# First layer's modulation: half of the products as fp32 matmuls of 512 columns, read back from diagonals

## The chip, the cores and the metric

The kernel runs on one core of a Trainium2 chip. The metric is the device time of one execution, in microseconds (us); every text here means that time when it says "time". The engines are TensorE (PE, with its weight loads shown apart as PEld), VectorE (DVE), ScalarE (ACT), GpSimd (POOL) and SyncE (SP), which issues most DMAs.

## The reference, cut to what matters

Four layers work on `x` of 1024 tokens by 1024 features. Each layer begins with a modulation that depends on the condition `c` alone:

```
cond = jax.nn.silu(c)                                     # (1, 1024)
for i in range(DEPTH):
    mod = (cond @ w_mod[i] + b_mod[i])[:, None, :]        # w_mod[i]: 1024 x 3072
    shift, scale, gate = jnp.split(mod, 3, axis=-1)
    h = rms_norm(x, norm_pre_g[i]) * (1.0 + scale) + shift
    o = mixer_i(h, ...)                                   # GLA, SGU, FoX, GLA
    x = x + gate * rms_norm(o, norm_post_g[i])
```

The change touches only how `shift` and `scale` of the first layer are computed, a product of one row of 1024 by a matrix of 1024 x 2048 in fp32. They are needed as columns: feature on the partition, one column for each block of 128 features.

## The kernel before, in words

`setup` loads the small vectors, transposes them with PE into `vec`, and makes `cond` (128 partitions x 8 columns: feature `128 kt + p` of silu(c) on partition p of column kt).

`begin` is the first layer's start. It holds the part that changes. It goes through four blocks of 512 columns of `w_mod[0]`, in the order j = 0, 2, 1, 3. Blocks 0 and 1 are the shift (`SH`), blocks 2 and 3 the scale (`G`, which becomes (1 + scale) times the norm's weight). In the texts the four are numbered in their order of arrival, w0 to w3: w0 is SH of features 0 to 511, w1 is G of the same features, w2 and w3 are SH and G of features 512 to 1023. One block comes in four DMAs of 512 KB (kp = 0 to 3), each with two row blocks of 128 (kt = 2 kp and 2 kp + 1), into a pool `whl` of eight buffers that the projection's split weights share.

`mod_pieces` with `wide=True` does the sum over the 1024 rows of a block in two places. DVE (L264) multiplies a row block by its column of `cond` and adds it into `acc` (128 x 512, which starts as zero with the bias in row 0), so that partition p holds a partial sum; PE (L274) then sums `acc` over the partitions with a column of ones, four matmuls of one column, which lands as columns in PSUM. Every fourth row block (kp odd, i = 1) goes to PE directly (L259): four matmuls whose weights are a 128 x 128 piece of `w_mod` and whose moving operand is the one column of `cond`. All go into one PSUM tile `pt` of the pool `pb` (two buffers), opened by a product with zeros (L243).

Between the blocks `begin` starts the first four token tiles (`first`): ACT takes the mean square and scales the tile (L425, L431, with POOL's L415 and L416 between them), PE transposes it (L443), and ACT copies the two PSUM halves out (L1261) into `raw`. When `SH` and `G` of a half are there, `entry_b` applies them to the four tiles of that half (ACT L457, for features 512 to 1023 partly DVE L454), ACT rounds to `hTh` (L462) and DVE, for the last one POOL, makes the rest `hTl` (L466). The first projection (L361, L362, L363: one product in three) needs both. ACT also splits the projection's weights (`whi` L321, `wlo` L323); for some of them the second part is finished by an accumulating DMA that POOL issues (L324).

The kernel is written with a scheduler: it orders each engine's instructions itself, except those that are pinned to the program's order (ACT's instructions of the first entry among them). So an engine's order can differ from the order of the code, and every engine works its list strictly in that order.

Of the kernel before, what the change touches and what calls it, by code (L numbers as in the profile page):

```python
# [8 lines left out]
F32 = mybir.dt.float32  # L9
# [3 lines left out]
ALU = mybir.AluOpType  # L13
AX = mybir.AxisListType

P = 128
# [78 lines left out]
class Trunk:  # L95
# [39 lines left out]
    def setup(self):  # L135
        nc, cp, a = self.nc, self.cp, self.a
        self.ident = cp.tile([P, P], F32, name="ident")
        make_identity(nc, self.ident)
        self.ones = cp.tile([P, P], F32, name="ones")
        nc.vector.memset(self.ones, 1.0)  # L140
        self.zero = cp.tile([P, 4], F32, name="zero")
        nc.vector.memset(self.zero, 0.0)
        self.half = cp.tile([P, 8], F32, name="neghalf")
        nc.vector.memset(self.half, -0.5)
        self.junk = cp.tile([P, 256], mybir.dt.bfloat16, name="junk")
        L = a["norm_pre_g"].shape[0]
        self.onesr = cp.tile([P, P], F32R, name="onesr")
        nc.vector.tensor_copy(self.onesr, self.ones)
        rows = self.s2([P])
        nc.vector.memset(rows, 0.0)  # L150
        n = 0
        self.vcol = {}

        def put(key, ap, cnt):
            nonlocal n
            nc.sync.dma_start(out=rows[n:n + cnt, 0:ap.shape[1]], in_=ap)
            self.vcol[key] = n
            n += cnt


        self.xts = [self.load_x(0)]
        put("c", a["c"].rearrange("b (k p) -> (b k) p", p=P), KT)
        put("gpre", a["norm_pre_g"].rearrange("l (k p) -> (l k) p", p=P), L * KT)
        self.xts.append(self.load_x(1))
        put("ghead", a["gla_g_head"].rearrange("l h (k p) -> (l h k) p", p=P), 2 * 8)
        put("ba", a["gla_b_a"].rearrange("l (k p) -> (l k) p", p=P), 2 * 4)
        self.xts.append(self.load_x(2))
        self.vcol["gq"] = n
        nc.sync.dma_start(out=rows[n:n + 1, 0:64], in_=a["fox_g_q"])
        nc.sync.dma_start(out=rows[n:n + 1, 64:128], in_=a["fox_g_q"])  # L170
        self.xts.append(self.load_x(3))
        self.vcol["gk"] = n + 1
        nc.sync.dma_start(out=rows[n + 1:n + 2, 0:64], in_=a["fox_g_k"])
        nc.sync.dma_start(out=rows[n + 1:n + 2, 64:128], in_=a["fox_g_k"])
        n += 2
        put("bf", a["fox_b_f"], 1)
        pt = self.ps("pm")
        nc.tensor.transpose(pt[:, 0:P], rows, self.ident)
        self.vec = cp.tile([P, P], F32, name="vec")
        nc.vector.tensor_copy(self.vec, pt[:, 0:P])  # L180
        c0 = self.vcol["c"]
        th = cp.tile([P, KT], F32, name="cth")
        nc.scalar.activation(th, self.vec[:, c0:c0 + KT], AF.Tanh, scale=0.5)
        nc.vector.scalar_tensor_tensor(th, th, 1.0, self.vec[:, c0:c0 + KT], op0=ALU.add, op1=ALU.mult)
        self.cond = cp.tile([P, KT], F32, name="cond")
        nc.vector.tensor_scalar(self.cond, th, 0.5, None, op0=ALU.mult)
        g0 = self.vcol["ghead"]
        self.ghalf = cp.tile([P, 16], F32, name="ghalf")
        nc.vector.tensor_scalar(self.ghalf, self.vec[:, g0:g0 + 16], 0.5, None, op0=ALU.mult)

        self.hTh = self.hp.tile([P, KT, SEQ], F32R, name="hTh")
        self.hTl = self.hp.tile([P, KT, SEQ], F32R, name="hTl")
        self.xd = [self.dp.tile([SEQ, D], F32, name=f"xd{i}") for i in range(max(1, len(self.layers) - 1))]
        self.yd = [self.dp.tile([SEQ, D], F32, name=f"yd{i}") for i in range(len(self.layers))]
        self.G = [None] * 4
        self.SH = [None] * 4
        self.gg = [None] * 4
# [25 lines left out]
    def mod_pieces(self, l, cols, wide=False):  # L223
        nc, a = self.nc, self.a
# [5 lines left out]
        G, SH, gg = self.G[l], self.SH[l], self.gg[l]  # L230
        pieces, ends = [], []

        def col(j):
            st = {}

            def begin():
                acc = self.sp.tile([P, 512], F32, tag="md", name=self.nm("md"), bufs=4)
                nc.gpsimd.memset(acc, 0.0)
                nc.sync.dma_start(out=acc[0:1, :], in_=a["b_mod"][l:l + 1, j * 512:(j + 1) * 512])
                st["acc"] = acc  # L240
                if wide:
                    st["pt"] = self.ps("pb")
                    nc.tensor.matmul(st["pt"][:, 0:4], self.ident, self.zero, start=True, stop=False)  # L243

            def step(kp):
                w = []
                if wide:
                    wt = self.wp.tile([P, 2, 512], F32, tag="whl", name=self.nm("md2"))
                    self.last["sp"] = nc.sync.dma_start(out=wt, in_=a["w_mod"][l, 2 * kp * P:(2 * kp + 2) * P, j * 512:(j + 1) * 512]
                                      .rearrange("(i p) n -> p i n", p=P))  # L250
                    w = [wt[:, i, :] for i in range(2)]
                else:
                    for i in range(2):
                        w.append(self.sp.tile([P, 512], F32, tag="md", name=self.nm("md"), bufs=4))
                for i in range(2):
                    kt = 2 * kp + i
                    if wide and kp % 2 and i:
                        for c in range(4):
                            nc.tensor.matmul(st["pt"][:, c:c + 1], w[i][:, c * P:(c + 1) * P], self.cond[:, kt:kt + 1],  # L259
                                             start=False, stop=False)  # L260
                        continue
                    if not wide:
                        nc.sync.dma_start(out=w[i], in_=a["w_mod"][l, kt * P:(kt + 1) * P, j * 512:(j + 1) * 512])
                    ins = nc.vector.scalar_tensor_tensor(st["acc"], w[i], self.cond[:, kt:kt + 1], st["acc"],  # L264
                                                         op0=ALU.mult, op1=ALU.add)
                    if not wide:
                        self.tc.keep_in_program_order(ins)

            def finish():
                acc = st["acc"]  # L270
                if j < 4:
                    pt = st["pt"] if wide else self.ps("pm")
                    for i in range(4):
                        self.last["tensor"] = nc.tensor.matmul(pt[:, i:i + 1], acc[:, i * P:(i + 1) * P], self.ones[:, 0:1],  # L274
                                                               start=not wide, stop=not wide or i == 3)
                    k0 = (j % 2) * 4
                    if j < 2:
                        nc.vector.tensor_copy(SH[:, k0:k0 + 4], pt[:, 0:4])
                    else:
                        g0 = self.vcol["gpre"] + l * KT + k0  # L280
                        nc.vector.scalar_tensor_tensor(G[:, k0:k0 + 4], pt[:, 0:4], 1.0, self.vec[:, g0:g0 + 4],
                                                       op0=ALU.add, op1=ALU.mult)
                else:
                    cs = (j - 4) * 512
                    gp = self.s2([512])
                    nc.sync.dma_start(out=gp, in_=a["norm_post_g"][l:l + 1, cs:cs + 512].partition_broadcast(P))
                    pt = self.ps("pm")
                    hi, lo = self.s2([512], F32R), self.s2([512], F32R)
                    nc.scalar.copy(hi, acc)
                    nc.gpsimd.tensor_tensor(lo, acc, hi.bitcast(F32), op=ALU.subtract)  # L290
                    nc.tensor.matmul(pt, self.onesr, hi, start=True, stop=False)
                    nc.tensor.matmul(pt, self.onesr, lo, start=False, stop=True)
                    nc.vector.tensor_tensor(gg[:, cs:cs + 512], pt, gp, op=ALU.mult)

            pieces.append(lambda: (begin(), step(0)))
            if ends:
                pieces.append(ends.pop())
            for kp in range(1, 4):
                pieces.append((lambda kp: lambda: step(kp))(kp))
            ends.append(finish)  # L300
            if wide or j == cols[-1]:
                pieces.append(ends.pop())
# [1043 lines left out]
```

## Time and profile before

| | us |
|---|---|
| median of 3 runs | 2137.44 |
| lowest, highest | 2134.9, 2142.99 |
| the profiled execution, its own time | 2137.6 |
| its span, first to last instruction | 2135.9 |
| PE busy in the span | 2069.4 (97%) |
| DVE, ACT, POOL busy | 1242.0, 956.5, 715.9 |

"Busy" counts the records of instructions; matmuls are pipelined, so PE busy does not mean PE at its peak. The span can be cut into stretches: up to 13.5 us the small loads, to 44.2 us the modulation, to 64 us the first projection that waits for pieces of the entry, and after that a long run in which PE is rarely without work. Of an fp32 matmul the trace has two records, of a product in fp32r or a transpose one.

### The profile page before, as it was taken

To read this page: it belongs to the slowest core of one execution; us is meant where nothing else is said; L and a number is where in the kernel's file an instruction comes from. 1 tells how busy PE (TensorE), PEld (TensorE's weight loads), DVE (VectorE), ACT (ScalarE), POOL (GpSimd) and SP (SyncE) were. 2 spreads that over 40 slices of the span, in tenths; PEclk is the share of its full clock that TensorE was granted. 3 is DMA by queue.
4 is the path that set the end of the run, shared out by engine and by line. 5 is a ranking of instruction groups with operands and counts; after the bars stand their busy time and mean duration, and the time that the engine had idled before them with its cause. 6 is when DMAs were issued, how large, how long until landed. Compare 5 with 4: busy or idle time off the path is not lost. (4 is left out here: it accounts for less than half of the span.)

```text
span 2135.9 us, 35845 instructions
## 1 busy us (share of the span) xinstructions
PE 2069.4 (97%) x13637; PEld 1847.1 (86%) x13637; DVE 1242.0 (58%) x2877; ACT 956.5 (45%) x1963; POOL 715.9 (34%) x730
## 2 busy tenths in 40 slices
PE   6999999999999999999999999999899899999998
PEld 6889999988998888898888888888687799899986
DVE  5476768545375425556656656656765554766542
ACT  5556445335321114554445445445555664543331
POOL 1422222345244322535343243343223321222251
PEclk9999999999999999999999999999999999999999
DMA  8344445434425433324223224223424542333422
GB/s 294 72 122 115 126 121 144 136 112 142 127 82 158 143 109 107 125 63 109 75 75 110 80 70 110 80 70 109 136 83 144 142 98 61 89 80 94 146 94 91
DMA packets 166965, 237.29 MB, mean 111 GB/s; under 512 B 14642, under 2 KB 97138, under 8 KB 166794
## 3 DMA queue, kind: packets, MB, share of 16 engines
q1 hardware_dynamic: 160170, 210.82, 31.4%
q0 software_dynamic: 6624, 24.19, 6.4%
q8 instruction: 107, 1.75, 0.3%
q14 instruction: 64, 0.52, 0.1%
HBM read 172.44 MB, written 29.95 MB: 95 GB/s over the span
## 5 line engine op out<-in xcount | busy, mean ns | idle before, releaser
L361 PE MATMUL pj<-whi,hTh 128*128 128x256 f32 (+1 forms) x2048 | 599.4, 293 | 6.2 <-ACT s L1047 2.7
L363 PE MATMUL pj<-whi,hTl 128*128 128x256 f32 (+1 forms) x2048 | 591.5, 289 | 0.5 <-DVE hTl L466 0.4
L362 PE MATMUL pj<-wlo,hTh 128*128 128x256 f32 (+1 forms) x2048 | 591.7, 289 | 0.0
L361 PEld LDWEIGHTS pj<-whi,hTh 128*128 128x128 f32 x2048 | 394.2, 192 | 13.2 <-issue 5.3
L362 PEld LDWEIGHTS pj<-wlo,hTh 128*128 128x128 f32 x2048 | 394.0, 192 | 5.0 <-issue 2.2
L363 PEld LDWEIGHTS pj<-whi,hTl 128*128 128x128 f32 x2048 | 393.9, 192 | 5.2 <-issue 2.2
L363 PE MATMUL pj<-hTh,wlo 128*128 128x512 f32 x640 | 253.4, 396 | 2.1 <-DMA wlo<-wraw 2.1
L361 PE MATMUL pj<-hTh,whi 128*128 128x512 f32 x640 | 255.2, 399 | 0.0
L362 PE MATMUL pj<-hTl,whi 128*128 128x512 f32 x640 | 252.5, 394 | 0.0
L326 POOL TENSOR_TENSOR wlo<-wraw,whi 128x1024 fp32r<-128x1024 f32 (+2 forms) x64 | 141.2, 2216 | 154.1 <-ACT whi L321 153.9
L264 DVE SCALAR_TENSOR_TENSOR md<-md,cond,md 128x512 f32<-128x512 f32 x184 | 161.2, 877 | 39.1 <-DMA md<-in_w_mod 37.3
L1120 POOL TENSOR_TENSOR db<-s,mneg 128x128 f32<-128x128 f32 x128 | 67.8, 537 | 276.5 <-DVE mx L1135 165.3
L321 ACT CAST whi<-wraw 128x1024 fp32r<-128x1024 f32 (+2 forms) x112 | 110.7, 989 | 95.3 <-PE pj L362 70.8
L1154 ACT COPY s<-pm 128x512 f32<-128x512 f32 (+2 forms) x192 | 87.5, 480 | 126.9 <-PE pm L1152 124.0
L363 PEld LDWEIGHTS pj<-hTh,wlo 128*128 128x128 f32 x640 | 120.7, 189 | 27.3 <-DMA wlo<-wraw 2.5
L361 PEld LDWEIGHTS pj<-hTh,whi 128*128 128x128 f32 x640 | 120.8, 189 | 23.7 <-issue 0.7
L362 PEld LDWEIGHTS pj<-hTl,whi 128*128 128x128 f32 x640 | 120.8, 189 | 23.6 <-issue 0.7
L1141 ACT ACTIVATE p<-p,ng 128x256 f32<-128x256 f32 (+7 forms) x128 | 99.5, 778 | 86.1 <-DVE ng L1139 85.1
L361 PE MATMUL pj<-wo,hTh 128*128 128x512 f32 x320 | 126.4, 396 | 1.7 <-ACT s L496 1.7
L362 PE MATMUL pj<-wo,hTh 128*128 128x512 f32 x320 | 125.2, 391 | 0.0
L363 PE MATMUL pj<-wo,hTl 128*128 128x512 f32 x320 | 123.5, 392 | 0.0
L1130 DVE CUSTOM_DVE_ANT_0 p<-pb,s 128x512 f32<-128x512 f32 (+3 forms) x160 | 82.4, 527 | 62.1 <-PE pb L1127 59.3
(223 smaller groups left out, 4072.7 us busy)
## 6 DMA issues: line engine op xcount, KB each, us to landing
md<-in_w_mod SPq DMA_DIRECT2D x160, 256.0 KB
wlo<-wraw POOLq DMA_DIRECT2D x44, 512.0 KB, 5.2
wraw<-in_gla_w_in SPq DMA_DIRECT2D x32, 512.0 KB
yd<-s SPq DMA_DIRECT2D x50, 256.0 KB
xd<-x SPq DMA_DIRECT2D x24, 512.0 KB
wraw<-in_sgu_w_in SPq DMA_DIRECT2D x24, 512.0 KB
x<-xd SPq DMA_DIRECT2D x24, 512.0 KB
wraw<-in_fox_w_in SPq DMA_DIRECT2D x48, 256.0 KB
```

The costliest lines, as they stand in the source:

```text
L264: ins = nc.vector.scalar_tensor_tensor(st["acc"], w[i], self.cond[:, kt:kt + 1], st["acc"], op0=ALU.mult, op1=ALU.add)
L321: nc.scalar.copy(hi, raw)
L326: getattr(nc, sub).tensor_tensor(lo, raw, hi.bitcast(F32), op=ALU.subtract)
L361: nc.tensor.matmul(ps, lh, rh, start=first, stop=False)
L362: nc.tensor.matmul(ps, lh, rl, start=False, stop=False)
L363: nc.tensor.matmul(ps, ll, rh, start=False, stop=last)
L1120: nc.gpsimd.tensor_tensor(db, nf[p, ib // 4, hb][:, qc], mneg, op=ALU.add)
L1130: nc.vector.tensor_tensor_reduce(e[:, c * 512:c * 512 + d0], sp[:, 0:d0], nf[p, c, hb][:, 0:d0], op0=ALU.add, op1=ALU.max, scale=1.0, scal ...
L1141: nc.scalar.activation(e[:, 0:n + P], e[:, 0:n + P], AF.Exp, bias=ng, accum_out=ls[:, 0:1])
L1154: nc.scalar.copy(et[:, 0:nb * P], pt[:, 0:nb * P])
```

## The change

For the four blocks of the first layer, and for them only:

- `crow` is new: the columns kt = 1, 3, 5, 7 of `cond`, each repeated 128 times, 4 x 128 x 128 in all, made by one DVE copy (L187).
- Of each kp the second row block (i = 1) goes to PE, now for all four kp. It is one fp32 matmul (L258) whose weights are the repeated condition and whose moving operand is the row block, 128 x 512. Every partition of `pt` then holds the same row of 512 sums. The first one opens `pt`; the product with zeros and its tile are gone.
- `acc` gets the four first row blocks (i = 0) on DVE as before, four L262 (L264 before) in place of six.
- At the end one fp32 matmul of `ones` (128 x 128) by `acc` (L275) adds its sums to the same `pt`, in place of four of one column.
- Since `pt` holds rows, the columns are picked out: for each 128 columns DVE multiplies `pt` by the identity and sums along the row (L278, `tensor_tensor_reduce`, whose sum is written by a second instruction), into `SH` or `G`. For `G` the step with the norm's weight then works on it in place (L288).

The other layers' blocks are as before. The diff, cut to this:

```diff
+        self.crow = self.s2([4, P])
+        nc.vector.tensor_copy(self.crow, self.cond.rearrange("p (k i) -> p k i", i=2)[:, :, 1:2].to_broadcast([P, 4, P]))
...
                 if wide:
                     st["pt"] = self.ps("pb")
-                    nc.tensor.matmul(st["pt"][:, 0:4], self.ident, self.zero, start=True, stop=False)
...
-                    if wide and kp % 2 and i:
-                        for c in range(4):
-                            nc.tensor.matmul(st["pt"][:, c:c + 1], w[i][:, c * P:(c + 1) * P], self.cond[:, kt:kt + 1],
-                                             start=False, stop=False)
+                    if wide and i:
+                        nc.tensor.matmul(st["pt"], self.crow[:, kp, :], w[i], start=kp == 0, stop=False)
                         continue
...
-                    for i in range(4):
-                        self.last["tensor"] = nc.tensor.matmul(pt[:, i:i + 1], acc[:, i * P:(i + 1) * P], self.ones[:, 0:1],
-                                                               start=not wide, stop=not wide or i == 3)
...
+                    col = (SH if j < 2 else G)[:, k0:k0 + 4]
+                    if wide:
+
+                        self.last["tensor"] = nc.tensor.matmul(pt, self.ones, acc, start=False, stop=True)
+                        dg = self.s2([4, P])
+                        for i in range(4):
+                            nc.vector.tensor_tensor_reduce(dg[:, i, :], pt[:, i * P:(i + 1) * P], self.ident, op0=ALU.mult,
+                                                           op1=ALU.add, scale=1.0, scalar=0.0, accum_out=col[:, i:i + 1])
```

The scheduler's order changes with it, in the first part of each engine's list; from there on the lists are the same but for one matmul of a later modulation that moves by some rows. Three places follow.

On DVE, the end of the modulation. `md_317` and `md_328` are w2's `acc`, `md_351` and `md_368` w3's. Before:

```order
L326 TENSOR_TENSOR wlo_365<-wraw_301,whi_364 128x1088
L281 SCALAR_TENSOR_TENSOR G_148<-pb_269,vec 128x4
L264 SCALAR_TENSOR_TENSOR md_328<-md_53_333,cond,md_328 128x512
L264 SCALAR_TENSOR_TENSOR md_328<-md_54_337,cond,md_328 128x512
L264 SCALAR_TENSOR_TENSOR md_328<-md_55_344,cond,md_328 128x512 x2
```

Now, where ISA is L278, two rows for each:

```order
L262 SCALAR_TENSOR_TENSOR md_351<-md_69_363,cond,md_351 128x512
L262 SCALAR_TENSOR_TENSOR md_351<-md_70_367,cond,md_351 128x512
L278 ISA s_51_281,G_148<-pb_263,ident 128x128
L278 ISA G_148 128x1
...
L278 ISA s_60_338,SH_149<-pb_320,ident 128x128
L278 ISA SH_149 128x1
...
L288 SCALAR_TENSOR_TENSOR G_148<-G_148,vec 128x4
L473 TENSOR_TENSOR hTl<-s_22_193,hTh 128x4x128
L278 ISA s_71_372,G_148<-pb_354,ident 128x128
```

`G` of the first half (`pb_269` before, `pb_263` now) stood ahead of nearly all of w2's sums; it now stands behind the last sum of w3.

On PE, from the first of w2's products on. Before:

```order
L259 MATMUL pb_331<-cond,md_54_337 128x1 x4
L243 MATMUL pb_371<-zero,ident 128x4
L259 MATMUL pb_331<-cond,md_56_348 128x1 x4
L443 MATMUL pm_252<-ident,x_112 128x128 x4
L443 MATMUL pm_257<-ident,x_112 128x128 x4
L274 MATMUL pb_331<-ones,md_328 128x1 x4
L259 MATMUL pb_371<-cond,md_64_377 128x1 x4
```

Now:

```order
L258 MATMUL pb_320<-md_59_333,s_7_124 128x512
L450 MATMUL pm_225<-ident,x_106 128x128 x4
L450 MATMUL pm_230<-ident,x_106 128x128 x4
L275 MATMUL pb_320<-md_317,ones 128x512
L450 MATMUL pm_246<-ident,x_110 128x128 x4
L450 MATMUL pm_251<-ident,x_110 128x128 x4
L258 MATMUL pb_354<-md_67_355,s_7_124 128x512
```

(`s_7_124` is `crow`; `x_112` and `x_110` are the fourth token tile.) The first tile's transposes moved too: before they were ahead of all products of the modulation, now they come behind w1's third product.

On SP, the first loads. Before:

```order
L826 DMA s_7_140<-in_gla_w_a 16x512 x3
L239 DMA md_150<-in_b_mod 1x512
L249 DMA md_11_155<-in_w_mod 128x2x512
L249 DMA md_12_159<-in_w_mod 128x2x512
L249 DMA md_13_166<-in_w_mod 128x2x512
L249 DMA md_14_170<-in_w_mod 128x2x512
L239 DMA md_266<-in_b_mod 1x512
```

Now:

```order
L240 DMA md_150<-in_b_mod 1x512
L249 DMA md_12_154<-in_w_mod 128x2x512
L249 DMA md_13_158<-in_w_mod 128x2x512
L249 DMA md_14_162<-in_w_mod 128x2x512
L249 DMA md_15_166<-in_w_mod 128x2x512
L240 DMA md_260<-in_b_mod 1x512
L833 DMA s_8_140<-in_gla_w_a 16x512 x3
```

Three small loads (`in_gla_w_a`, which ACT's second instruction reads, ahead of the first token tile) moved from ahead of w0 to behind it; the second token tile's load moved behind two small ones.

## Rows read from the trace of the kernel before

**Rows 1.** The page's head and first part: busy time, share, instructions.

```profile
span 2135.9 us, 35845 instructions
...
PE 2069.4 (97%) x13637; PEld 1847.1 (86%) x13637; DVE 1242.0 (58%) x2877; ACT 956.5 (45%) x1963; POOL 715.9 (34%) x730
```

**Rows 2.** Windows: stretch, its length, busy by engine (instructions), clock, DMA share, GB/s.

```profile
13.50:44.20 30.70, 28.04 (x132) 27.87 (x133) 21.24 (x30) 19.54 (x31) 3.18 (x7) 1.00 1.00 334
```

**Rows 3.** Timeline of ACT: start, us, instruction, count, idle before and its releaser.

```profile
19.41 1.15 ACT L431 ACTIVATE x<-x,r 128x1024 f32<-128x1024 f32 x1 [0.95 <-POOL r L416]
...
37.83 1.65 ACT L457 ACTIVATE s<-s,SH,G 128x128 f32<-128x128 f32 x4
...
56.09 0.62 ACT L462 CAST hTh<-s 128x512 fp32r<-128x512 f32 x1
```

**Rows 4.** Timeline of POOL, end of the first entry.

```profile
56.78 1.29 POOL L466 TENSOR_TENSOR hTl<-s,hTh 128x512 fp32r<-128x512 f32 x1 [22.68 <-ACT hTh L462]
...
58.95 1.99 POOL L324 DMA_DIRECT2D wlo<-wraw  x2
```

**Rows 5.** Timeline of PE, modulation and first projection.

```profile
14.82 1.97 PE L443 MATMUL pm<-ident,x 128*128 128x128 f32 x8 [4.33 <-ACT x L431]
...
23.30 1.71 PE L259 MATMUL pb<-cond,md 128*128 128x1 f32 x8
...
35.34 1.97 PE L443 MATMUL pm<-ident,x 128*128 128x128 f32 x8 [1.05 <-ACT x L431]
...
44.61 0.43 PE L362 MATMUL pj<-wlo,hTh 128*128 128x272 f32 x1
44.84 0.43 PE L363 MATMUL pj<-whi,hTl 128*128 128x272 f32 x1
...
47.71 0.29 PE L361 MATMUL pj<-whi,hTh 128*128 128x272 f32 x1
47.83 0.29 PE L362 MATMUL pj<-wlo,hTh 128*128 128x272 f32 x1
...
63.75 0.50 PE L363 MATMUL pj<-hTh,wlo 128*128 128x512 f32 x1 [2.06 <-DMA wlo<-wraw]
...
65.32 0.63 PE L362 MATMUL pj<-hTl,whi 128*128 128x512 f32 x1
65.75 0.63 PE L363 MATMUL pj<-hTh,wlo 128*128 128x512 f32 x1
```

**Rows 6.** Timeline of DVE in the modulation.

```profile
13.57 2.33 DVE L264 SCALAR_TENSOR_TENSOR md<-md,cond,md 128x512 f32<-128x512 f32 x3 [1.24 <-DMA md<-in_w_mod]
...
18.93 2.33 DVE L264 SCALAR_TENSOR_TENSOR md<-md,cond,md 128x512 f32<-128x512 f32 x3 [0.39 <-DMA md<-in_w_mod]
...
27.86 0.75 DVE L264 SCALAR_TENSOR_TENSOR md<-md,cond,md 128x512 f32<-128x512 f32 x1 [0.37 <-DMA md<-in_w_mod]
...
40.20 1.54 DVE L264 SCALAR_TENSOR_TENSOR md<-md,cond,md 128x512 f32<-128x512 f32 x2
```

**Rows 7.** Timeline of PE later: two fp32 matmuls of 256 columns.

```profile
394.85 0.59 PE L789 MATMUL pm<-st,s 128*128 128x256 f32 x2
395.28 0.59 PE L790 MATMUL pm<-s,s 128*128 128x256 f32 x2
```

**Rows 8.** Timeline of DVE later: a multiply-and-reduce of 128 columns out of PSUM.

```profile
1442.76 0.29 DVE L1135 CUSTOM_DVE_ANT_0 p<-pb,db 128x128 f32<-128x128 f32 x1
1442.97 0.08 DVE L1135 DVE_READ_ACCUMULATOR2_ANT mx<- 128x1 f32 x1
1442.97 0.75 DVE L264 SCALAR_TENSOR_TENSOR md<-md,cond,md 128x512 f32<-128x512 f32 x1
```

**Rows 9.** Timeline of SP's queue, modulation loads.

```profile
9.31 1.93 SPq L249 DMA_DIRECT2D md<-in_w_mod  x4
...
30.57 0.37 SPq L249 DMA_DIRECT2D md<-in_w_mod  x1
...
32.93 1.75 SPq L249 DMA_DIRECT2D md<-in_w_mod  x2
```

More of the change, by code (lines that the diff above doesn't have):

```diff
@@ L140, in setup @@
         nc.vector.memset(self.ones, 1.0)
-        self.zero = cp.tile([P, 4], F32, name="zero")
-        nc.vector.memset(self.zero, 0.0)
         self.half = cp.tile([P, 8], F32, name="neghalf")
@@ L272, in finish @@
                     pt = st["pt"] if wide else self.ps("pm")
-                    for i in range(4):
-                        self.last["tensor"] = nc.tensor.matmul(pt[:, i:i + 1], acc[:, i * P:(i + 1) * P], self.ones[:, 0:1],
-                                                               start=not wide, stop=not wide or i == 3)
                     k0 = (j % 2) * 4
-                    if j < 2:
-                        nc.vector.tensor_copy(SH[:, k0:k0 + 4], pt[:, 0:4])
-                    else:
+                    col = (SH if j < 2 else G)[:, k0:k0 + 4]
[5 more added lines that the diff above has]
+                                                           op1=ALU.add, scale=1.0, scalar=0.0, accum_out=col[:, i:i + 1])
+                    else:
+                        for i in range(4):
+                            nc.tensor.matmul(pt[:, i:i + 1], acc[:, i * P:(i + 1) * P], self.ones[:, 0:1],
+                                             start=True, stop=True)
+                    if j < 2 and not wide:
+                        nc.vector.tensor_copy(col, pt[:, 0:4])
+                    elif j >= 2:
                         g0 = self.vcol["gpre"] + l * KT + k0
-                        nc.vector.scalar_tensor_tensor(G[:, k0:k0 + 4], pt[:, 0:4], 1.0, self.vec[:, g0:g0 + 4],
+                        nc.vector.scalar_tensor_tensor(col, col if wide else pt[:, 0:4], 1.0, self.vec[:, g0:g0 + 4],
                                                        op0=ALU.add, op1=ALU.mult)
```

## The prediction

> **What bounds the kernel now.** I read the page's first part first: PE is busy 2069.4 of 2135.9 us [rows 1], so outside some 66 us nothing but fewer or faster products of PE shortens the run, and the change takes no work from the long part. It acts in one place, so the rest is read there. The windows view of 13.5 to 44.2 us [rows 2] shows the modulation: PE busy 28.0 of 30.7 us, DVE 21.2, ACT 19.5, and the DMA engines at a share of 1.00 with 334 GB/s. Three things look like a bound, and the busy shares can't tell which it is.
>
> PE's busy time there is cheap work: eight records of one-column products take 1.71 us, 0.21 us each [rows 5]. The clock column says 1.00, but the durations contradict it: at 44.6 us the first products of 272 columns follow each other in 0.23 us, and at 47.7 us, after some 3 us of such products without a pause, in 0.12 us [rows 5]. [...] For PE in this stretch the durations count, not the column.
>
> DVE waits for data at each block: 13.57 (w0), 18.93 (w1), 27.86 (w2) are starts released by DMA [rows 6]. w0 to w1 is 5.36 us, 1.34 us for a DMA of 512 KB.
>
> What sets the end of the stretch is found backwards from the first long wait of PE in the projection: 2.06 us up to 63.75 for a `wlo` that an accumulating DMA finishes [rows 5]. POOL issues that DMA at 58.95, behind its `hTl` of the last tile at 56.78, which waits for ACT's last `hTh` at 56.09 [rows 3, 4]. ACT gets there by one list of modulate and round steps that begins at 37.83 and is nearly unbroken, 18.9 us to 56.7. **So the price of the change is how far the start of that list, 37.83, moves.** Behind 64 us PE is the bound and what it loses ahead it doesn't get back.
>
> **The change part by part.**
>
> *DVE's sums.* Of 24 steps of 0.75 us [rows 6], 8 go: 6.0 us less. Added are 16 multiply-and-reduce steps. The nearest rows are those of 128 columns out of PSUM with max in place of sum: 0.29 us plus 0.08 for the write of the result, and the next instruction starts 0.21 us after the first began [rows 8]. Between 0.21 and 0.37 each, 3.4 to 5.9 us; I take 0.25, since the trace's instructions overlap: 4.0 us. The net gain of DVE is 0.1 to 2.6 us, but DVE waited for data there anyway, so I count nothing for it. The copy into `crow` lies between 0.3 us and 0.75 us (a DVE pass of 512 fp32 [rows 6]); it runs while w0 is still on its way, as long as that lands after some 11.9 us.
>
> *PE's products.* Out go 32 products of one column and the 16 of the sums, 96 records of 0.21 us, 20.5 us, and 4 with zeros. In come 20 fp32 products of 512 columns. The trace has none of that width with two records; two of 256 columns start 0.43 us apart at the full clock [rows 7], so 0.86 us for 512, and at half the clock 1.71. The bill of PE is 17 us at the one and 34 us at the other level, in a stretch of 30.7 us that also holds 32 transposes (7 to 8 us at half clock, by eight records in 1.97 [rows 5]). Which level it is decides the case. These products stream columns without a pause, like those at 44.6, so I expect the rise within a few us of the first. Then each product (0.86) is shorter than its DMA (1.34), PE waits for data, and may fall back: after the 2.06 us of idling before 63.75 the products of 512 columns at 65.3 again follow each other in 0.43 us [rows 5]. It will swing, with the busy half in its favour.
>
> [...]
>
> *The loads.* The three small loads go behind w0, and w0's first DMA can go before 9.31 [rows 9]. I take 1.7 us, since `cond` and `crow` aren't there before about 11.9; the bounds are 0 and 2.3. Then w0 to w2 keep their distances, since transfers set them: w2's first piece at 26.2 in place of 27.86, its last three pitches later, 30.2. ACT's second instruction now waits for the small loads behind w0: about 16 us. So the first token tile is squared and scaled by about 20 us in place of 14.8.
>
> *ACT's tiles.* From one tile's transposes (14.82) to the next one's scaled tile it takes 5.7 us (19.41 plus 1.15 [rows 3, 5]), and the four came in 6.8 us each because PE had other work (14.82 to 35.34). Now the first transposes stand behind w1's third product, which lands near 20: 20.8. Three steps of 5.4 to 5.9 give the fourth tile's transposes at 37.1 to 38.6, in place of 35.34. They were followed by the start of ACT's list after 2.5 us (35.34 to 37.83), which is 2.0 at full clock: **39.1 to 41.1**.
>
> *G behind w3.* The other condition for that start. `G` of the first half was read long before w3's end; now its four steps and the four of w2's `SH` stand on DVE behind w3's last sum. w3's buffers come free when both DVE and PE have used w2's: first DMA issued at 30.57 before, the last by 34.7, and the last sum ended at 41.74 (40.20 plus 1.54), 7.0 us later [rows 6, 9]. Now the last goes out when w2's last product is done, 30.2 plus 0.9, and the last sum ends at 36.3 (four pitches after w2's last, and 0.75) to 38.1 (7.0 after its issue). With 8 steps of 0.25 and the small step of 0.16: **38.5 to 40.3**. The same reading frees a `pb` buffer, so w3's five products on PE can't begin before; their sums are needed only some 10 us after ACT's start, since ACT has its list of the first half ahead of them: five products of 1.71, 8.6 us, and 1.2 of DVE fit, hardly.
>
> *Sum.* ACT's list starts at the later of the two, 39.1 to 41.1; I take 40.7, near the end with PE at the lower level for part of the time, 2.9 us later than 37.83. The list keeps its 18.9 us, POOL's DMA and PE's wait go with it. What PE saves by being warm at 44 (some 1.4 us) lies ahead of pieces that it then waits for. The profiled execution took 2137.6 us; 2137.6 plus 2.9 is **2140.5 us**, slower than the median of 2137.44 by 0.14%.
>
> **The rivals.**
>
> *PE stays at its lower level (slower).* Speaks for it: it did so for 30 us with a busy share of 0.9 [rows 2]. Against: those were one-column products. Eight products of 1.71 (w0's five, w1's three) put the first transposes at 25.6, and w2's last product at 39.4, after six more products and two tiles' transposes of 1.75 each; w3's last sum ends 7.0 later, 46.4, and G is there at 48.6. The list starts 10.8 us late: 2148.4 us. It decides from the point where a product is longer than its DMA of 1.34 us for most of the 20.
>
> *The earlier loads win.* If the small loads are what held w0, and PE is warm from the first block on, both chains end at their early bounds or a little ahead, 37.0 to 39: from 0.8 us faster to 1.2 slower, 2136.8 to 2138.8. No path gives more, since ACT's list and all behind it stay.
>
> *The new products cost nothing.* If ACT's tiles were the only bound before and now (the fourth's transposes at 35.34 waited 1.05 us for ACT [rows 5]), the change would do nothing of what it says for the time: only the moved order of the tiles would count, 2 us: 2139.6. It gives nearly the forecast's time and differs in what the start waits for: ACT's own copies, not G.
>
> **How the numbers follow.** Forecast (the two chains, 1 to 5 us later) 0.61; early loads 0.15; nothing but the tiles 0.08; PE at the lower level 0.10, about half of it over the bound below; what I don't see, to either side alike, 0.06. A difference of 0.5%, 10.7 us, is about what a measurement of this kernel can tell from no change. Faster by more: 0.03, since no part can give 10.7 us; slower by more: 0.08; within: 0.89. The range: the early case less the scatter of the runs (some 3 us), 2133, up to PE's lower level, 2148.
>
> **What would show it.** Right: L258's two records 0.85 us from one product to the next in w1 and w2, ACT's list starting at 39 to 41 with G's last step just ahead, the length of the list unchanged, and the DMA of `wlo` moved by the same. Wrong: products 1.71 us apart up to w3 (the slow rival); the first w_mod sum not before 13.5; multiply-and-reduce steps of over 0.4 us, which would put 8 of them on the path at once; or a difference at the end that isn't there at 64 us, which would mean that the long part doesn't carry a shift through.

## The result, and the profile after

The changed kernel took 2150.76 us (median of 5 runs, 2148.96 to 2153.26), the kernel before 2137.44 us (2133.27 to 2142.99); the ratio is 1.0056, with a 95% interval of 1.0039 to 1.0074. It is 13.3 us slower, where 2140.5 had been forecast and 2133 to 2148 given as the range. The profiled execution has a span of 2149.4 us, 13.5 more than [rows 1]. The page of the changed kernel, its head and two of its DMA queues (packets, MB, share of 16 engines):

```profile
span 2149.4 us, 35742 instructions
...
PE 2074.5 (97%) x13573; PEld 1837.2 (85%) x13573; DVE 1240.7 (58%) x2899; ACT 955.6 (44%) x1963; POOL 717.0 (33%) x730
...
q8 instruction: 107, 1.75, 0.4%
q14 instruction: 65, 0.53, 0.1%
```

PE has 64 records of products and 64 of weight loads fewer and is busy 5 us longer. In the first layer it is busy less (44.3 us up to 66.5, before 46.0 up to 64.25). So the work behind it, which the change leaves alone, ran slower.

**The first layer.** DVE's timeline of the changed kernel (start, duration, work, and in brackets the wait ahead of it) answers [rows 6, 8]:

```profile
12.65 0.75 DVE L262 SCALAR_TENSOR_TENSOR md<-md,cond,md 128x512 f32<-128x512 f32 x1 [0.65 <-DMA md<-in_w_mod]
...
38.83 0.75 DVE L262 SCALAR_TENSOR_TENSOR md<-md,cond,md 128x512 f32<-128x512 f32 x1 [0.66 <-DMA md<-in_w_mod]
39.50 0.28 DVE L278 CUSTOM_DVE_ANT_0 s<-pb,ident 128x128 f32<-128x128 f32 x1
39.70 0.08 DVE L278 DVE_READ_ACCUMULATOR2_ANT G<- 128x1 f32 x1
39.70 0.29 DVE L278 CUSTOM_DVE_ANT_0 s<-pb,ident 128x128 f32<-128x128 f32 x1
...
41.18 0.16 DVE L288 SCALAR_TENSOR_TENSOR G<-G,vec 128x4 f32<-128x4 f32 x1
```

The multiply-and-reduce steps follow each other in 0.21 us and stand behind w3's last sum. ACT's timeline, against [rows 3]:

```profile
39.20 1.26 ACT L1268 COPY s<-pm 128x512 f32<-128x512 f32 x2 [0.75 <-PE pm L450]
41.38 1.65 ACT L464 ACTIVATE s<-s,SH,G 128x128 f32<-128x128 f32 x4 [0.92 <-DVE G L288]
...
58.33 0.62 ACT L469 CAST hTh<-s 128x512 fp32r<-128x512 f32 x1
```

ACT's list starts at 41.38, released by `G`'s last step, and was at 37.83 before. It ends at 58.95 (58.33 plus 0.62), 2.2 us later than before. PE's timeline, against [rows 5]:

```profile
12.68 6.68 PE L258 MATMUL pb<-md,s 128*128 128x512 f32 x8 [2.11 <-DMA md<-in_w_mod]
...
20.05 2.74 PE L258 MATMUL pb<-md,s 128*128 128x512 f32 x6
22.63 1.04 PE L450 MATMUL pm<-ident,x 128*128 128x128 f32 x8
...
38.51 1.33 PE L450 MATMUL pm<-ident,x 128*128 128x128 f32 x8 [3.53 <-ACT x L438]
40.48 6.45 PE L258 MATMUL pb<-md,s 128*128 128x512 f32 x8 [0.64 <-DVE G L278]
...
66.02 0.50 PE L370 MATMUL pj<-hTh,wlo 128*128 128x512 f32 x1 [1.20 <-DMA wlo<-wraw]
```

Two records are one product (the 20 of the first layer have 40). w0's four took 6.68 us and w3's 6.45, 1.6 to 1.7 us each, those of w1 and w2 some 0.9. I read this as two levels of PE's clock: the windows view has a granted clock of 0.50 from 39.2 to 46.0 us (w3) and 1.00 from 18.7 to 39.2; w0's products lie ahead of the trace's first entry of the clock, at 18.7, where the view has 1.00, and are as long as w3's. The wait for `wlo` ends at 66.02, 2.27 us later than [rows 5]. So far the forecast holds: 2.9 us had been worked out.

**Behind the first layer.** I matched PE's products of each run with those of the kernel before, and took how much later the same product starts (us; columns are moments in the kernel before; negative is earlier). A row is one profile, and six profiles of kernels whose work is that of before lie between 0 and -2.8 at 217. The last four kernels are explained below.

| kernel | 66 | 217 | 660 | 700 | 920 | 1300 | 1470 | 1760 | end |
|---|---|---|---|---|---|---|---|---|---|
| changed | 1.8 | -1.3 | -1.3 | 1.1 | 2.3 | 4.0 | 8.3 | 13.7 | 13.8 |
| p127d | 2.8 | 1.5 | 1.5 | 1.5 | 1.5 | 0.7 | 0.4 | 0.9 | 1.0 |
| q129d | 3.8 | 2.6 | 2.5 | 2.5 | 3.6 | 6.1 | 9.8 | 15.6 | 15.5 |
| s1 | -2.4 | -5.2 | -4.4 | -2.1 | -0.9 | -0.4 | 2.2 | 4.3 | 4.3 |
| s127d | -2.7 | -3.9 | -3.9 | -3.9 | -2.9 | -4.1 | -3.0 | -3.9 | -3.8 |

At 217 us the changed kernel was ahead of the kernel before in this profile. It loses 15.0 us between 660 us and 1760, in layers whose instructions are the same and, but for one summing product that stands 33 triples of products away, in the same order. Two windows of PE's clock tell how. The windows view (busy us of the engines, granted clock, DMA share, GB/s), first of the kernel before, then of the changed one:

```profile
1290.00:1550.00 260.00, 251.90 (x1944) 215.79 (x1943) 168.35 (x550) 130.39 (x286) 91.56 (x97) 0.99 0.33 98
```

```profile
1290.00:1550.00 260.00, 250.85 (x1881) 217.38 (x1880) 162.96 (x523) 125.31 (x271) 92.00 (x97) 0.95 0.31 89
```

PE is as busy in both, and the second has 63 records of products fewer in its 260 us, at a mean clock of 0.95 instead of 0.99: 0.04 of 260 us is 10.4 us, about what the table shows for this stretch (1.3 us late at 1215, 10.7 at 1540). Behind 100 us the changed kernel has 27 us more at half clock than before, and 4.7 us more of waits of PE (43.0 against 38.3). Each of its eight stretches of half clock between 900 and 1800 us begins within 2 us behind a wait of PE of 1.0 to 2.7 us; that at 1462 is shown below. The question of the study was where these waits come from.

### The profile page after: what moved, and what is told of

Same layout as the page of the kernel before. It is cut to its first block, busy times and chain, and to the rows that moved or that the text cites. A ratio compares the mean times of both kernels' runs of the same rounds, so it can differ in the third digit from the quotient of the medians.

```text
span 2149.4 us, 35742 instructions
## 1 busy us (share of the span) xinstructions
PE 2074.5 (97%) x13573; PEld 1837.2 (85%) x13573; DVE 1240.7 (58%) x2899; ACT 955.6 (44%) x1963; POOL 717.0 (33%) x730
## 3 DMA queue, kind: packets, MB, share of 16 engines
q8 instruction: 107, 1.75, 0.4%
## 5 line engine op out<-in xcount | busy, mean ns | idle before, releaser
L262 DVE SCALAR_TENSOR_TENSOR md<-md,cond,md 128x512 f32<-128x512 f32 x176 | 156.6, 891 | 45.9 <-DMA md<-in_w_mod 44.3
L1246 ACT ACTIVATE s<-pj 128x256 f32<-128x256 f32 (+1 forms) x96 | 43.7, 456 | 169.5 <-PE pj L370 161.5
```

The source lines that it names most:

```text
L1246: nc.scalar.activation(dst, ps, AF.Tanh, scale=0.5)
```

## Experiments

**Twice the same, and five turns of a buffer ring (b2, a2, r1, s1).** Two theories first. A: the change ends the first layer at another moment, and the clock then falls at other places. B: something of the change lasts, such as the turns of the `s2` ring (`crow` and the four `dg` are five tiles). r1 is the kernel before with five turns and no other work:

```
+        nc.vector.memset(self.s2([4, P])[:, 0, 0:1], 0.0)
...
+                    if wide:
+                        nc.vector.memset(self.s2([4, P])[:, 0, 0:1], 0.0)
```

s1 is the changed kernel without turns, which also moves work in the first layer:

```
-        self.crow = self.s2([4, P])
-        nc.vector.tensor_copy(self.crow, self.cond.rearrange("p (k i) -> p k i", i=2)[:, :, 1:2].to_broadcast([P, 4, P]))
...
-                        nc.tensor.matmul(st["pt"], self.crow[:, kp, :], w[i], start=kp == 0, stop=False)
+                        nc.tensor.matmul(st["pt"], self.cond[:, kt:kt + 1].to_broadcast([P, P]), w[i], start=kp == 0, stop=False)
...
-                        dg = self.s2([4, P])
+                        dg = self.junk.rearrange("p (i t) -> p i t", t=P)
...
```

Expected of b2:

> The kernel before once more, as a second trace of it. Theory A (behind 66 us the order of the instructions is the same in both kernels, and the 11 us come from where TensorE's clock falls to its lower level, which a shift of a few us in the first layer moves): the falls behind 100 us stand elsewhere than in the first trace or have another sum than its 17 us, and the time follows them, 2132 to 2146 us. Theory B (something of the change holds on behind the first layer, such as the five more turns of the ring of small buffers): the same places and the same sum of falls, 2133 to 2143 us.

Of a2:

> The changed kernel once more, as a second trace. Theory A: falls of the clock behind 100 us at other places than in its first trace, the sum between 17 and 50 us, time 2138 to 2153 us. Theory B: the same places as in its first trace (1298, 1462, 1524, 1534, 1691, 1756 us, sum 44 us), 2149 to 2153 us.

Of r1:

> The kernel before with five more small buffers taken from the ring in the first layer, as the change does, each with one tiny memset on DVE and nothing else; PE, ACT and SP keep the order of before. Theory B (the turned ring): 2146 to 2152 us, ratio 1.004 to 1.007. Theory A: the first layer is the same within 1 us, and the rest is as good as before's, 2133 to 2143 us, ratio 0.998 to 1.003.

Of s1:

> The changed kernel without the five turns of the ring: the repeated condition is read as a column repeated by its address instead of a copy, and the products of the diagonal step go to a scrap tile. The scheduler then places G of the first half earlier. Theory B (the turned ring): back to within 0.2% of before, 2134 to 2142 us. Theory A: first layer's wait for wlo ends at 63 to 66 us, the rest adds between 0 and 12 us by where the clock falls: 2136 to 2152 us, not tied to the ring.

Measured: b2 2137.53 us (ratio 1.0002, 0.9989 to 1.0014), a2 2150.93 (1.0064, 1.0043 to 1.0085), r1 2137.47 (1.0003, 0.9992 to 1.0015), s1 2141.53 (1.0019, 1.0006 to 1.0033). So the difference comes back, and r1 puts the ring out. The second traces have 27 us of half clock behind 100 us for the kernel before, leaving out the fall at the very end (17 in the first trace), and 41 for the changed one (44), in part at other moments: in a2 one stands at 1216 where the first trace has none. s1's time lies in the range of both theories and decides nothing; its trace speaks against theory A: its first layer is 5.2 us earlier at 217 us, and yet it loses 2.3 us near 690, 1.2 near 910, 2.6 near 1460 and 2.4 near 1750, at the same products as the changed kernel. That these losses keep their place in the program when the moment moves says that they aren't made by the moment.

**A place where the loss begins.** The first of these is a step of DVE that sums a later modulation. DVE's timelines, of the kernel before, then of the changed one:

```profile
670.02 2.31 DVE L264 SCALAR_TENSOR_TENSOR md<-md,cond,md 128x512 f32<-128x512 f32 x3
675.39 1.42 DVE L264 SCALAR_TENSOR_TENSOR md<-md,cond,md 128x512 f32<-128x512 f32 x2 [3.06 <-DMA md<-in_w_mod]
```

```profile
668.73 2.31 DVE L262 SCALAR_TENSOR_TENSOR md<-md,cond,md 128x512 f32<-128x512 f32 x3
675.70 1.43 DVE L262 SCALAR_TENSOR_TENSOR md<-md,cond,md 128x512 f32<-128x512 f32 x2 [4.65 <-DMA md<-in_w_mod]
```

SP issued the transfers alike (1.3 us earlier in the changed kernel, as everything was), and they land 1.6 us later against that. The DMA view of 671 to 677 us (busy tenths and GB/s in 40 slices, queues below), before and changed:

```profile
DMA  9989826796799999999999999742200000000000
GB/s 410 314 287 382 266 48 109 177 266 191 266 341 328 335 307 369 362 423 396 369 403 437 423 396 396 273 164 109 82 27 0 0 0 0 0 0 0 0 0 0
...
q1 hardware_dynamic: 955, 1.30, 64.2%
```

```profile
DMA  9889999999999988632120000000000000000000
GB/s 341 266 287 321 355 375 389 376 417 410 430 423 423 396 328 314 260 123 82 48 48 0 14 14 14 27 27 14 27 27 27 14 0 0 0 0 0 0 0 0
...
q1 hardware_dynamic: 745, 0.98, 46.5%
q8 instruction: 1, 0.02, 1.1%
```

Before, the transfers end together. In the changed kernel most have ended at the 21st slice, but a trickle of 14 to 27 GB/s goes on for ten slices of 0.15 us, as of one or two of the page's 16 engines that are behind (an estimate: one packet of 2 KB in 0.08 us is 25 GB/s). And there is one packet of the kind "instruction", 16 KB, which took 1.06 us, from 672.88 to 673.93; packets of 2 KB beside it took 0.08, and from 674.1 to 675.8 they run one behind the other. The page counts 107 of these 16 KB packets in both kernels, 1.75 MB (`q8 instruction: 107, 1.75, 0.3%` before). I read them as PE's program, fetched while it runs: they start between 31 and 2095 us of the trace of before, and from one start to the next PE, with its weight loads, begins 256 instructions in the mean of either trace (161 to 344), of 27,579 before and 27,452 in the changed kernel. A piece is then 256 instructions of 64 bytes, an estimate from 16 KB and this count. The change takes 127 instructions out of PE's program ahead of everything else, so by this reading every border between pieces moves by half a piece against the work. Theory D: **at its new place a piece's transfer stands ahead of data that PE or DVE waits for.**

**Padding with empty instructions (p127, q129, q256, q64).** The first trial of theory D put empty instructions ahead of the program (127 in the changed kernel, 129, 256 and 64 in the kernel before):

```
+    for _ in range(127):
+        nc.tensor.nop(nofuse=True)
```

> The changed kernel with 127 empty instructions on PE ahead of the program, as many as the change took out of PE's stream; the order of the work on every engine is that of the changed kernel. PE's program comes to the chip in pieces of 16 KB by DMA (107 in the trace of before, one about every 20 us, 0.9 to 1.4 us each); the change shifted where their borders lie. Theory D (one of these pieces meets a transfer that PE waits for): with the borders back where before has them the waits of PE near 694 (2.1 us), 910 (1.4), 1461 (1.7) and 1754 us (2.0) go back to before's (under 0.3, 0.24, 0.3, 1.3), and the time is 2139 to 2142 us. Theory A (the clock falls because the first layer ends at another moment): 2150 us, as the changed kernel. Either with some us for the empty instructions themselves.

> The kernel before with 129 empty instructions on PE ahead of the program: the borders of the 16 KB pieces of PE's program then lie where the changed kernel has them (127 fewer instructions, or 129 more, of 256 to a piece). Theory D: the waits of the changed kernel appear, near 694, 910, 1457 and 1744 us, with none of the change, and the time is 2144 to 2150 us. Theory A: 2137.5 us, as the kernel before. Either with some us for the empty instructions themselves.

> The kernel before with 256 empty instructions on PE ahead of the program, a whole piece: the borders lie where they were. Both theories: 2137.5 us plus what the empty instructions cost themselves, so this run gives that cost (0 to 10 us; twice that of 127 or 129).

> The kernel before with 64 empty instructions on PE ahead of the program, a quarter of a piece. Theory D: the pieces are fetched at other moments than in either kernel, so the time is its own, anywhere between 2135 and 2151 us, with PE's waits at other places. Theory A: 2137.5 us. Either with a quarter of the cost that 256 empty instructions have.

Measured: p127 2151.46 us (ratio 1.0051, 1.0031 to 1.0071), q129 2137.90 (0.9991, 0.9980 to 1.0001), q256 2136.52 (0.9988, 0.9978 to 0.9998), q64 2138.78 (0.9996, 0.9983 to 1.0009). It looks like the end of theory D and isn't. The traces have as many instructions as without the padding (35742 in p127 and the changed kernel, 35845 in the other three and the kernel before), and the pieces come at the same places: near 674 us in the moments of the kernel before for p127 and the changed kernel, near 686 for the others. The empty instructions are not in the program that ran. These are four more runs of the two kernels, and they show only that the difference comes back.

**Padding with drains, and the addresses (p127d, q129d, zc).** Drain instructions stayed in the program (35869 instructions in p127d, 127 more than the changed kernel). They were put into PE's finished list, so that no other instruction changes its place, where PE waits for data anyway:

```
+    blocks = nc.main_func.blocks
+    have = len(blocks[-1].instructions)
+    for i in range(n):
+        nc.tensor.drain(fusable=False)
+    pads = blocks[-1].instructions[have:]
+    del blocks[-1].instructions[have:]
+    work = blocks[1].instructions
+    at = [i for i, x in enumerate(work) if x.opcode == "Matmult"][0]
+    work[at:at] = pads
```

In the changed kernel they go ahead of PE's first product (the index `[0]`), in the kernel before behind the two products with zeros (`[2]`).

p127d is the changed kernel with 127 of them, so that its borders lie where before has them; q129d is the kernel before with 129, so that its borders lie where the changed kernel has them. The traces show it: the piece near 674 comes near 686 in p127d, that near 686 comes near 673 in q129d. zc tries a third cause, theory C: the change removes a tile of 16 bytes per partition, so later tiles lie at other addresses. It puts the tile back:

```
+        self.zero = cp.tile([P, 4], F32, name="zero")
+        nc.vector.memset(self.zero, 0.0)
```

> The changed kernel with 127 drain instructions on PE ahead of its first transpose, where PE waits for data until 10.1 us anyway; they are in PE's program of 64-byte instructions (27,583 as in the kernel before, where the changed kernel has 27,456), and the order of all other instructions is that of the changed kernel. So the borders of the 16 KB pieces in which PE's program is fetched lie again where before has them, behind the first layer. Theory D (at its present places a piece of program meets transfers that PE waits for): PE's waits near 694, 910, 1461 and 1754 us go back to before's (0.3, 0.2, 0.3 and 1.3 us), and the time is 2137 to 2142 us. Theories A and B: 2150 us, with these waits, as the changed kernel.

> The kernel before with 129 drain instructions on PE between its products with zeros and its first transpose, where PE waits until 10.0 us anyway; order of all else as before. The borders of the 16 KB pieces then lie where the changed kernel has them (256 instructions to a piece; 127 fewer or 129 more is the same place). Theory D: the changed kernel's waits of PE appear near 694 (2 us), 910 (1.4), 1457 (1.7) and 1744 us (2.0) without any of the change, and the time is 2143 to 2150 us. Theories A and B: 2137.5 us, as the kernel before.

> The changed kernel with the tile of four zeros per partition and its memset put back (nothing reads it), so that every later tile lies at the address that it has in the kernel before; the order on PE, ACT and POOL is that of the changed kernel. Theory C (addresses in SBUF moved by the removed tile make later transfers or reads slower): 2137 to 2142 us. Theory D and the rest: 2150 us, as the changed kernel.

Measured: **p127d 2140.47 us** (ratio 1.0011, 1.0002 to 1.0020), **q129d 2152.14** (1.0067, 1.0050 to 1.0083), zc 2149.93 (1.0057, 1.0045 to 1.0070). Theory C is out. The kernel before takes on the changed kernel's time, without any of the change, when its borders are moved, and the changed kernel loses most of its surplus when they are moved back. Of q129d's 13.3 us over the kernel before in the same round (2138.80) some 2.6 were there at 217 us, since the 129 drains took 9.4 us of PE and held its first transpose from 10.04 to 13.33; the other 10.7 come behind that, at the changed kernel's later places but the one near 694 (table above). q129d's time is 2 us above the range expected of it.

A wait of PE for a transfer `s<-s` of 128 KB shows it closest. PE's timelines of before, changed, p127d and q129d:

```profile
1456.90 0.30 PE L1126 MATMUL pb<-s,s 128*128 128x128 f32 x1 [0.28 <-DMA s<-s]
```

```profile
1462.28 0.30 PE L1133 MATMUL pb<-s,s 128*128 128x128 f32 x1 [1.74 <-DMA s<-s]
```

```profile
1457.50 0.30 PE L1133 MATMUL pb<-s,s 128*128 128x128 f32 x1 [0.23 <-DMA s<-s]
```

```profile
1464.00 0.45 PE L1126 MATMUL pb<-s,s 128*128 128x128 f32 x1 [1.31 <-DMA s<-s]
```

The queues in the 10 us up to this wait (DMA view), before, changed, p127d, q129d:

```profile
q1 hardware_dynamic: 1325, 2.39, 91.5%
```

```profile
q1 hardware_dynamic: 1281, 2.31, 84.0%
q8 instruction: 1, 0.02, 0.6%
```

```profile
q1 hardware_dynamic: 1340, 2.42, 89.7%
```

```profile
q1 hardware_dynamic: 1304, 2.34, 77.5%
q8 instruction: 1, 0.02, 0.6%
```

In these four the two with a piece in this window wait 1.3 to 1.7 us, those without 0.2 to 0.3. Over all 16 traces the rule is looser. PE's wait at five places, and what a profile loses between 217 us and its end (us; places are moments in the kernel before):

| borders as in | traces | 695 | 909 | 1209 | 1457 | 1743 | lost |
|---|---|---|---|---|---|---|---|
| changed | changed, a2, p127, zc, s1 | 2.0 to 2.3 | 1.4 to 1.6 | 0.4 to 2.0 | 1.3 to 2.7 | 2.0 to 2.6 | 9.6 to 19.4 |
| changed | q129d | 0 | 1.4 | 2.0 | 1.3 | 2.1 | 12.9 |
| before | before, b2, r1, q129, q256, q64, p127d | 0 | 0.2 to 1.3 | 0.3 to 0.4 | 0 to 0.5 | 1.3 to 1.4 | -0.5 to 4.3 |
| before | s127d | 0 | 1.2 | 0.3 | 1.4 | 1.4 | 0.1 |
| a quarter off | q64d, p63d | 0 | 0.3, 1.1 | 0.3 | 0 | 1.3, 1.4 | 4.1, 5.0 |

What a profile loses goes with the borders in every trace, and so does the wait at 1743. That at 909 is also there in q129, q256, s127d and p63d, and that at 1457 in s127d, which has no piece in the 10 us up to it:

```profile
1453.82 0.30 PE L1131 MATMUL pb<-s,s 128*128 128x128 f32 x1 [1.36 <-DMA s<-s]
```

Ahead of the waits at 909 and 1743 the kernels with the changed kernel's borders have no piece of PE's program nearer than 22 and 19 us. So at these two a piece that stands ahead of the awaited data is not what the traces show. In the changed kernel SP had issued the four transfers 3.92 us later than before, as much as everything was late there, and PE's product started 5.38 us later; the granted clock then fell to half from 1462.6 to 1469.4, and the shift grew to 8.3. A landing 1.46 us later so cost 4.4. In s127d the clock didn't fall behind its 1.36 us, and the wait cost 1.1. The windows view of 1290 to 1550 for p127d and q129d, against 0.99 and 0.95 above:

```profile
1290.00:1550.00 260.00, 252.19 (x1955) 216.47 (x1954) 170.05 (x552) 132.09 (x289) 92.31 (x99) 1.00 0.34 99
```

```profile
1290.00:1550.00 260.00, 252.96 (x1910) 219.15 (x1908) 166.32 (x528) 126.50 (x274) 93.33 (x99) 0.96 0.32 93
```

**Two more places of the borders, and s1 padded (q64d, p63d, s127d).** The same edit with 64 drains in the kernel before (a quarter of a piece), with 63 in the changed kernel (three quarters), and with 126 in s1 (its borders as before):

> The kernel before with 64 drain instructions on PE ahead of its first transpose: the borders of the pieces a quarter of a piece from before's place. Theory D: the waits of q129d (near 911, 1211, 1463 and 1755 us) are gone or elsewhere, and the time is its own, anywhere from 2135 to 2151 us; with it the run tells whether the place of the kernel before is a lucky one (this one near 2150) or that of q129d an unlucky one (this one near 2138). The drains themselves lie in PE's wait (0.074 us each in q129d, 4.7 us together, of 6.2).

> The changed kernel with 63 drain instructions on PE ahead of its first transpose: the borders three quarters of a piece from before's place, a quarter from its own. The same question from the other side: anywhere from 2138 to 2153 us; near 2140 says that the changed kernel's own place is the unlucky one, near 2150 that the place of before is the lucky one.

> The changed kernel with the weights of the wide products read from one column of the condition at a repeated address (no copy) and the scrap of the multiply-and-reduce steps in a tile that is there, as in s1, plus 126 drain instructions on PE ahead of its first transpose, so that the borders of the pieces of PE's program lie behind the first layer where the kernel before has them (27,583 instructions). s1 is 4.7 us ahead of the kernel before at 217 us, loses 8 us behind it and ends at 2141.5. Theory D: the loss behind 217 us goes, and the time is 2131 to 2135 us, faster than both kernels. If the loss has another cause: 2141.5 us, as s1.

Measured: q64d 2140.90 us (ratio 1.0013, 1.0002 to 1.0024), p63d 2140.46 (1.0013, 1.0004 to 1.0022), **s127d 2133.78** (0.9979, 0.9970 to 0.9987). At three of the four places the times are 2137.4 to 2140.9 (before's place with both kernels, each quarter with one of them); the half piece is the one that costs. So of these four the changed kernel had the unlucky place, not the kernel before a lucky one. In s127d the 9.5 us that s1 loses behind 217 us don't come (table; 8 in the expectation), and it is faster than both kernels. Its first layer, in the timelines of DVE, ACT and PE:

```profile
29.92 0.15 DVE L286 SCALAR_TENSOR_TENSOR G<-G,vec 128x4 f32<-128x4 f32 x1
```

```profile
35.77 1.65 ACT L462 ACTIVATE s<-s,SH,G 128x128 f32<-128x128 f32 x4
```

```profile
61.57 0.50 PE L368 MATMUL pj<-hTh,wlo 128*128 128x512 f32 x1 [0.65 <-DMA wlo<-wraw]
```

Without the copy into `crow` and the ring tiles (the two were not tried apart), the scheduler places the first tile's transposes at 15.21 and `G` at 29.92, long before ACT needs it; ACT's list starts at 35.77 and the wait for `wlo` ends at 61.57, 2.2 us ahead of [rows 5].

## Why the prediction was wrong, point by point

- **The small loads and the first sum**: taken as 1.7 us earlier, at most 2.3; measured 12.65 against 13.57, 0.9. Right in direction, too large.
- **PE's products and their clock**: 0.86 or 1.71 us had been worked out and a swing between the levels foreseen; measured 0.86 to 0.9 in w1 and w2 and 1.6 to 1.7 in w0 and w3. Right. That w0's block would run at the lower level throughout (four products in 6.68 us) had not been counted on: PE worked from 12.68 to 22.63 without a pause, and the first transposes came at 22.63 instead of 20.8 (ACT's tile for them was scaled at 21.66).
- **Multiply-and-reduce**: 0.25 taken between 0.21 and 0.37; measured 0.21.
- **ACT's tiles**: the fourth tile's transposes at 37.1 to 38.6; measured 38.51.
- **`G` behind w3**: 38.5 to 40.3; measured 41.34, since w3's last sum ended at 39.58 instead of 36.3 to 38.1: w2's last product started at 31.91 instead of 30.2, and w3's last load left SP at 33.4 instead of 31.1. `G` is what released ACT, 0.92 us after its last copy. The rival in which the new products cost nothing named ACT's own copies, and falls.
- **The start of ACT's list**: 40.7 forecast, 39.1 to 41.1; measured 41.38. **The list's length** unchanged at 18.9 us: it was 17.6, so 1.3 of the 3.55 us came back there, and the wait for `wlo` ended 2.27 later, not 2.9.
- **The step that failed** is "It acts in one place, so the rest is read there": the assumption that no part of the change reaches the later layers, so that "Behind 64 us PE is the bound and what it loses ahead it doesn't get back" gives the end from the shift at 64 us. The sum and the range rest on both. What the runs showed in its place: the number of instructions in PE's program is part of the change. It moves the borders of the later pieces (the 33rd packet began at 672.9 us, at 659.8 before), and that costs about 10 us of 2150.76 behind 217 us (2140.47 with the borders put back). The prediction counted what the removed products took in time and not that they are 127 instructions ahead of 107 pieces; the row that shows those pieces was on the page of the kernel before, as a queue with 0.3% of the DMA engines' time.
- **What PE gets back**: this part of the step held in the main. In the changed kernel's first profile the 2.27 us were gone at 110 us, since the stretch from 64 to 217 us ran at a granted clock of 1.00, before at 0.98. But that is one profile: in the five profiles of the changed first layer (changed, a2, p127, zc, p127d) the shift at 217 us is -1.3, 1.8, 0.8, 1.6 and 1.5, and in the six of the first layer of before (before, b2, r1, q129, q256, q64) between 0 and -2.8. The medians lie 3.4 us apart at 66 us and 2.3 at 217, so about 1 us came back.
- **The one-sided rivals**: the slow rival (PE at its lower level through the modulation, 2148.4) gave nearly the time that came, by a mechanism that didn't happen. The prediction's own test tells them apart, "a difference at the end that isn't there at 64 us", and that is what the trace shows.
- **The size**: with the borders where before has them the changed kernel takes 2140.47 us, by the ratio 0.4 to 4.3 us more than before; the forecast was 2140.5. So close a hit is luck: the interval is 3.9 us wide, and ACT's list began 0.7 us later than forecast and was 1.3 shorter. The remaining 10 us are the borders.

What stays open: that the place of the borders makes the loss is shown, by moving them in three kernels. How it does so is shown in part. A piece among late data was followed in the trace at two places (676 and 1461 us). The wait at 1755 us (1743 in the table) goes with the borders, that near 911 (909) only in part, and ahead of both the changed kernel has no piece near; what is late there was not traced. The wait near 694 that was expected of q129d didn't come: the data of the step at 676 landed 0.9 us late in q129d, 1.6 in the changed kernel, and in q129d PE had no wait behind it. q129d lost 2 us in a wait near 1211 where the changed kernel lost none; a2, p127 and zc did too, and why is open. To move a single border wasn't tried.

## What to carry to other kernels

Here an edit that took 127 instructions out early in a long unrolled program also moved the later borders of the fetched program (the 33rd packet from 659.8 us to 672.9) and cost about 10 us behind 217 us. When a trace shows losses in code that nobody touched, at the same places whatever the start, compare the positions of the "instruction" packets and repeat the measurement with padding instructions that stay in the program (64 to 129 drains here) before judging the change. Where PE was busy for 97% of the span, data 1.46 us late cost 4.4 us: behind the wait at 1462 us the granted clock was 0.50 for 6.8 us. The price of such an edit is known only over several places of the borders: here the edit itself costs 0.4 to 4.3 us at the place of before, and a variant of it, padded to that place, gains 0.2%; neither was timed at all four.

## What the runs showed of the hardware

- A 16 KB packet of program took 0.9 to 2.2 us in the 16 traces (0.88 to 1.42 in the first of before, 0.88 to 1.76 in the first of the changed kernel), beside 0.08 us of most 2 KB packets of data, and data that was waited for landed 1.5 to 1.6 us late at the two places of the changed kernel where one fell among it (0.9 in q129d at the first).
- Of four places of the borders one costs 8 to 11 us more than before's (changed kernel against p127d 10.3, q129d against before 10.7 without its drains' 2.6, s1 against s127d 7.8).
- Empty instructions were not in the program that ran (35742 instructions in p127 as without them); drains on PE are (35869 in p127d) and took 0.073 us each, by an estimate from the 9.44 us that PE was idle over q129d's 129.
- fp32 products of 512 columns took 0.86 to 0.9 us at a granted clock of 1.00 (w1 and w2) and 1.6 at 0.50 (w3), and 1.67 in w0, ahead of the trace's first entry of the clock; with the weights read from one column at a repeated address (s1, s127d) they took no longer (six records in 2.74 us in s127d at 16.75, as in the changed kernel at 20.05).
